# Handing the experts' rows over to the next mixer: weights requested early, row sums on DVE, the gate applied at the scatter, a fixed order, and the overflow block's second half under a branch

## The chip, the cores and the metric

The program runs on one core of a Trainium2 chip. The metric is device time in microseconds (us), from the start of the program to its end. The engines are TensorE (PE in the rows, PEld for its weight loads), VectorE (DVE), ScalarE (ACT), GpSimd (POOL) and SyncE (SP, which here only issues DMAs). Each works through its own list of instructions in order and waits for the others on semaphores.

## What is computed

Two stacked blocks of a transformer, all in float32. The first has two layers, each a mixer followed by a mixture of experts; then comes a norm, and then a second block of its own two mixers, each followed by a convolutional feed-forward net. The parts that matter here:

```python
def modulate(x, g, shift, scale):
    return rmsnorm(x, g) * (1 + scale) + shift
...
for l in range(DEPTH):                       # DEPTH = 2
    h_l = modulate(x_lat, norm_mix[l], sh1, sc1)     # and h_c for the context tokens
    o_c, o_l = mixer_ab(...) if l % 2 == 0 else mixer_na(...)
    x_lat = x_lat + g1 * o_l
    h_l = modulate(x_lat, norm_ffn[l], sh2, sc2)
    # layer 0: 256 context + 512 latent tokens; layer 1: the latent ones alone
    y = hier_moe(tokens, ...)                # 32 experts, 2 per token
    x_lat = x_lat + g2 * y[n_c:]             # context: x_ctx + g2c * y[:n_c]
return rmsnorm(x_lat, norm_final)            # then second_block, which begins with even_mixer
...
(jax.nn.silu(xb @ w_gate[e]) * (xb @ w_up[e])) @ w_down[e]      # one expert
```

## The kernel before

Tokens lie in tiles of 128 rows of 1024 in `xO`: tiles 0 and 1 are the context, 2 to 5 the latent tokens. `moe` runs a layer's experts. Each expert has up to 128 tokens gathered by an indirect DMA (`ex_load`), transposed (`ex_x`, L1227), multiplied by its up and gate weights (`ex_in`, L1218) in halves of 64 tokens, passed through silu and product (`ex_act`, L1240 on ACT, L1241 on DVE), transposed (L1251, copied by DVE, L1252), multiplied by the down weights, scaled by each token's weight `wl` (layer 0: ACT, L1259; layer 1: DVE, L1261, where the gate row `gain` is multiplied in too) and scattered to `Y` (L1262), which holds two rows for each token. `experts` runs the 32 in order; a branch (L1299) reads from `tix` whether an expert has over 64 tokens and takes the arm with both halves (`ex_rest`) or that with the first alone (`ex_out`). Weights come through a ring of slots (`wraw`, L110), twelve of 512 KB for an expert, requested by SyncE. Tokens beyond an expert's 128 rows go to overflow blocks, run by a hardware loop of `nov` passes (L1095), which always computes both halves; `nov` was 1 in layer 0 and 0 in layer 1 here. `gains`, at the end of `experts`, spreads rows over 128 partitions with matmuls (L403, copied at L404): the gate rows `G` in layer 0, the final norm's row in layer 1.

`finish` hands over to the next mixer: `tile(t)` loads a tile's pairs of rows (`yp`, L1114, by SyncE), adds the two rows of a token (L1116, GpSimd), multiplies by the gate in layer 0 (L1118, DVE) and adds to `xO` (L1119, DVE). In `mixer_na` `norm(t)` squares (L312, ACT), takes the root (L294, ACT, which needs a table of its own, hence a table load), the reciprocal (L295, DVE), scales (L315, DVE) to `h`, and turns `h` on TensorE (L1394 for the shift, L1395), split into a high half (L197, ACT) and a low half (L198, DVE); the values projection (L202 to L204) follows tile by tile, then the others. `final_norm` does the like for `even_mixer` (transposes at L1554). The mixers' weights pass through `wchunk`: L121 on ACT makes the high half, L122 on DVE the low one.

What sets the order: the program's order on each engine, except that a scheduler may move an instruction that isn't kept in place by `keep_in_program_order`. `warm` (L194) issues matmuls whose result nobody reads. The loop's branch and its end stand on every engine's list.

## Time and profile before

| | before |
|---|---|
| median of 3 runs | 3548.57 us (3546.37 to 3550.68) |
| the profiled execution | 3547.91 us |
| its span | 3546.1 us |
| TensorE busy | 3280.6 us (93%) |
| DVE, ACT, GpSimd busy | 1464.9, 1052.8, 499.1 us |
| experts of layer 0 | about 622 to 1196 us |
| experts of layer 1 | about 1655 to 2181 us |

The profile is of one execution. Busy time is a mean over stages with different limits: in most of the experts the weights' DMAs set the pace, in the mixers TensorE does. What a change at one place is worth is read there, from which wait ends last.

### The profile page before, as it was taken

Reading aid. Unit: us, or ns where it says so; the run is one execution under the profiler, and the core shown is the slowest. Engines: PE = TensorE matmul, PEld = TensorE weight load, DVE = VectorE, ACT = ScalarE, POOL = GpSimd, SP = SyncE. Lnnn points to the kernel's source line nnn. Section 1 sums busy time; section 2 is a strip of 40 time slices with the busy share of each in tenths; the row PEclk is TensorE's granted clock in tenths of the full one; section 3 lists DMA queues with packets and bytes.
Section 4 is the critical chain, followed back from the end, with each engine's and each line's share of the span. In section 5 each row is a group of like instructions: output and inputs, shape, how many; then the busy total and the mean of one; then the engine's idle time right before and its main releaser. Section 6 shows DMA issues by size and latency. Waiting matters only on the chain. (4 is left out here: it accounts for less than half of the span.)

```text
span 3546.1 us, 44389 instructions
## 1 busy us (share of the span) xinstructions
PE 3280.6 (93%) x16488; PEld 2125.4 (60%) x16488; DVE 1464.9 (41%) x2831; ACT 1052.8 (30%) x1948; POOL 499.1 (14%) x581
## 2 busy tenths in 40 slices
PE   7999988999988799998988886999999999999998
PEld 5954556333322487765332222876888888788887
DVE  4476565211111455565211113427443456355344
ACT  3465541111111244451000001326332334333232
POOL 1044421111110223321111112103000000000000
PEclk9999999999999799999999998999999999999999
DMA  5134465998999422236999996323333344233331
GB/s 201 54 123 133 159 214 200 351 408 315 378 398 388 172 72 77 66 131 237 406 401 395 395 391 224 119 89 91 89 97 99 84 62 95 72 101 103 95 98 45
DMA packets 351078, 676.27 MB, mean 191 GB/s; under 512 B 43029, under 2 KB 194773, under 8 KB 349409
## 3 DMA queue, kind: packets, MB, share of 16 engines
q1 hardware_dynamic: 313816, 626.50, 50.3%
q0 software_dynamic: 17584, 25.94, 2.1%
q10 hardware_dynamic: 19416, 20.34, 1.9%
q8 instruction: 165, 2.70, 0.3%
q14 instruction: 97, 0.79, 0.1%
HBM read 676.74 MB, written 29.45 MB: 199 GB/s over the span
## 5 line engine op out<-in xcount | busy, mean ns | idle before, releaser
L1218 PE MATMUL ea<-wr,xT 128*64 128x512 f32 x2368 | 622.1, 603 | 47.8 <-DMA wr<-in_moe_w_up_dram 26.5
L122 DVE TENSOR_TENSOR wh<-wr,wh 128x1024 fp32r<-128x1024 f32 (+2 forms) x276 | 339.1, 1235 | 314.1 <-ACT wh L121 313.4
L202 PE MATMUL aw<-hh,wh 128*128 128x512 f32 (+1 forms) x1216 | 441.9, 364 | 3.7 <-ACT wh L121 2.6
L203 PE MATMUL aw<-hl,wh 128*128 128x512 f32 (+1 forms) x1216 | 442.5, 364 | 1.8 <-DVE hl L198 1.8
L204 PE MATMUL aw<-hh,wh 128*128 128x512 f32 (+1 forms) x1216 | 441.3, 364 | 0.0
L1218 PEld LDWEIGHTS ea<-wr,xT 128*64 128x64 f32 x2368 | 183.6, 137 | 427.7 <-issue 311.2
L121 ACT CAST wh<-wr 128x1024 fp32r<-128x1024 f32 (+2 forms) x276 | 281.3, 1027 | 433.5 <-PE acc L204 288.1
L1218 PE MATMUL ea<-wr,aT 128*64 128x512 f32 x1184 | 282.4, 619 | 44.2 <-DVE aT L1252 39.0
L203 PEld LDWEIGHTS aw<-hl,wh 128*128 128x128 f32 x1216 | 231.2, 190 | 40.0 <-issue 3.5
L202 PEld LDWEIGHTS aw<-hh,wh 128*128 128x128 f32 x1216 | 230.7, 190 | 40.9 <-ACT wh L121 3.5
L204 PEld LDWEIGHTS aw<-hh,wh 128*128 128x128 f32 x1216 | 231.0, 190 | 38.0 <-issue 3.5
L472 POOL TENSOR_TENSOR pp<-pp,rc 128x768 f32<-128x768 f32 (+3 forms) x192 | 211.7, 1110 | 259.1 <-DVE rc L471 244.9
L1218 PEld LDWEIGHTS ea<-wr,aT 128*64 128x64 f32 x1184 | 83.4, 141 | 188.0 <-issue 130.3
L1262 POOL DMA_INDIRECT Y<-ey,idx x74 | 74.7, 1010 | 859.9 <-ACT ey L1259 434.0
L470 ACT ACTIVATE pp<-s,nm 128x768 f32<-128x768 f32 (+3 forms) x192 | 137.1, 716 | 156.5 <-DVE nm L1486 79.5
L202 PE MATMUL acc<-wh,hh 128*128 128x512 f32 (+2 forms) x480 | 177.2, 369 | 0.0
L203 PE MATMUL acc<-wh,hh 128*128 128x512 f32 (+2 forms) x480 | 175.8, 366 | 0.0
L204 PE MATMUL acc<-wh,hl 128*128 128x512 f32 (+2 forms) x480 | 175.5, 366 | 0.0
L1252 DVE COPY aT<-pt 128x256 f32<-128x256 f32 x74 | 31.4, 424 | 329.1 <-PE pt L1251 329.1
L1228 ACT COPY xT<-pt 128x512 f32<-128x512 f32 x65 | 37.9, 583 | 388.4 <-PE pt L1227 376.1
L1228 DVE COPY xT<-pt 128x512 f32<-128x512 f32 x65 | 44.9, 691 | 248.8 <-PE pt L1227 248.8
L1240 ACT ACTIVATE sg<-ea 64x256 f32<-64x256 f32 x148 | 55.7, 376 | 300.7 <-PE ea L1218 248.8
(480 smaller groups left out, 5251.6 us busy)
## 6 DMA issues: line engine op xcount, KB each, us to landing
wr<-in_moe_w_gate_dram SPq DMA_DIRECT2D x260, 512.0 KB
wr<-in_moe_w_up_dram SPq DMA_DIRECT2D x260, 512.0 KB
wr<-in_moe_w_down_dram SPq DMA_DIRECT2D x260, 512.0 KB
wr<-in_w_ada_dram SPq DMA_DIRECT2D x96, 512.0 KB
wr<-in_ffn_w_up_dram SPq DMA_DIRECT2D x88, 512.0 KB
wr<-in_ffn_w_down_dram SPq DMA_DIRECT2D x44, 512.0 KB
wr<-in_odd_w_in_dram SPq DMA_DIRECT2D x32, 512.0 KB
wr<-in_na_w_in_dram SPq DMA_DIRECT2D x30, 512.0 KB
```

The source lines that it names most:

```text
L121: keep(self.nc.scalar.copy(hi, raw))
L122: keep((self.lo_eng or self.nc.vector).tensor_sub(lo, raw, f(hi)))
L202: mm(ps, ah, bh, start=first, stop=False)
L203: mm(ps, ah, bl, start=False, stop=False)
L204: mm(ps, al, bh, start=False, stop=last)
L470: nc.scalar.activation(p[:, :n], s[:, b:b + n], AF.Exp, bias=nm, scale=sign, accum_out=rc)
L472: nc.gpsimd.tensor_mul(p[:, :n], p[:, :n], rc.broadcast_to([P, n]))
L1218: self.tc.keep_in_program_order(self.nc.tensor.matmul(*a, **k))
L1228: (self.nc.vector.tensor_copy if g else self.nc.scalar.copy)(x[:, g * 4:g * 4 + 4, :], pt.rearrange("p (k t) -> p k t", t=P))
L1240: self.nc.scalar.activation(sg[64:, c], a[:64, c], AF.Silu)
L1252: nc.vector.tensor_copy(at, pt[:, :256].rearrange("p (k t) -> p k t", k=4))
L1262: nc.gpsimd.indirect_dma_start(Y.rearrange("t (h d) -> (t h) d", h=2), bass.IndirectOffsetOnAxis(ap=idx[:, h], axis=0), y, None, bounds_ch ...
```

## The change

- `overflow()` is called inside `experts` at the last one: it reads `nov`, requests the overflow block's weights under a branch, and then requests the first weight chunks of the next mixer (three for `mixer_na`, four for `even_mixer`), so that they stand ahead of the last branches on SyncE's list.
- The overflow block stands under `If(nov > 0)` and has the two arms of an expert; further blocks are a loop under `If(nov > 1)`.
- In layer 0 the gate is applied before the scatter: `ctx` says for each row whether its token is of the context, `dgain` is the difference of the two gate rows, and DVE does two products in place of ACT's one. `gains` spreads the next norm's rows there in place of the gate rows, and the spread after the loop is gone. `shift_scale` is done at the fourth expert.
- The two rows of a token are added by DVE; four `yp` loads are issued at once. `table` loads the root's table ahead.
- The norms of `mixer_na` and `even_mixer` are taken apart (`square`, `scale`, `turn`) and their instructions on DVE, ACT, TensorE and SyncE are kept in program order (they all show as line L52). Six `warm` matmuls stand ahead of the first turn: in `mixer_na` behind the first `add` (they read its result), in `even_mixer` ahead of all adds.

```diff
+class Pinned:
+    def __init__(self, tc, eng):
+        self.tc, self.eng = tc, eng
+    def __getattr__(self, name):
+        fn = getattr(self.eng, name)
+        def call(*a, **k):
+            return self.tc.keep_in_program_order(fn(*a, **k))
+        return call
...
+    def table(self, fn):
+        t = self.sm.tile([P, 1], F32, name="tab")
+        self.nc.scalar.activation(t, self.eps[EPS], fn)
...
-        if self.gain is None:
-            nc.scalar.mul(y, acc, wl[:, h])
-        else:
-            nc.vector.scalar_tensor_tensor(y, acc, wl[:, h], self.gain, ALU.mult, ALU.mult)
+        wl, ctx = wl
+        gain = self.gain
+        if ctx is not None:
+            gain = y
+            nc.vector.scalar_tensor_tensor(y, self.dgain, ctx[:, h], self.gain, ALU.mult, ALU.add)
+        nc.vector.scalar_tensor_tensor(y, acc, wl[:, h], gain, ALU.mult, ALU.mult)
...
             def gains():
                 if l:
                     self.gfin = self.spread(pg, src, 8, ps, "xg1")
-                    return
-                for i, w in enumerate(ws):
-                    G[w] = self.spread(pg, src, 8 * i, ps, f"xg{i}")
-            past = self.past(nt, sc["K"], idx, tix, wl, eid, px, ps, off)
+                else:
+                    self.nA = {w: self.spread(pg, self.nmod[0], 16 * w + 8, ps, f"xg{i}") for i, w in enumerate(ws)}
+            past = self.past(nt, sc["K"], idx, tix, wl, eid, px, ps, off, ctx)
             def first():
-                self.both(idx[:, :, :NE], slf, ps, off)
+                self.both(idx[:, :, :NE], slf, ps, off, None if l else ctx[:, :, :NE])
...
+            def overflow():
+                nov = nc.values_load(eid[0:1, NOB:NOB + 1], min_val=0, max_val=NOB)
+                ev = nc.sync.value_load(eid[0:1, 0:1], min_val=0, max_val=NE - 1)
+                self.n = RING - 1
+                with tc.If(nov > 0):
+                    w = self.ex_load_w(l, ev)
                 self.n = -1
-                self.shift_scale()
-            with tc.For_i(0, nov, 1):
-                ev = nc.sync.value_load(eid[0:1, 0:1], min_val=0, max_val=NE - 1)
-                self.expert(l, ev, idx[:, :, NE:NE + 1], wl[:, :, NE:NE + 1], xo, Y, T, px, ps)
-                for a, w0 in ((tix, NE), (idx[:, 0], NE), (idx[:, 1], NE), (eid, 0), (wl[:, 0], NE), (wl[:, 1], NE)):
-                    sh = px.tile([P, NOB - 1], a.dtype, name="sh", tag="sh")
-                    nc.vector.tensor_copy(sh, a[:, w0 + 1:w0 + NOB])
-                    nc.vector.tensor_copy(a[:, w0:w0 + NOB - 1], sh)
-                self.ex_load(tix[:, NE:NE + 1], xo, hD, T)
+                self.raws = [self.wraw(s) for s in then]
+                return nov, w
+            nov, w = self.experts(l, tix, idx, wl, ctx, xg, hD, Y, T, px, ps,
+                                  [first] + past + ([] if l else [self.shift_scale]), gains, overflow)
+            with tc.If(nov > 0):
+                self.ex_block(w, xo, slots, px, ps, nc.values_load(tix[64:65, NE:NE + 1], min_val=0, max_val=int(BIG)))
+            self.n = RING + 11
+            with tc.If(nov > 1):
+                with tc.For_i(1, nov, 1):
+                    for a, w0 in ((tix, NE), (idx[:, 0], NE), (idx[:, 1], NE), (eid, 0), (wl[:, 0], NE), (wl[:, 1], NE),
+                                  *([] if l else [(ctx[:, 0], NE), (ctx[:, 1], NE)])):
+                        sh = px.tile([P, NOB - 1], a.dtype, name="sh", tag="sh")
+                        nc.vector.tensor_copy(sh, a[:, w0 + 1:w0 + NOB])
+                        nc.vector.tensor_copy(a[:, w0:w0 + NOB - 1], sh)
+                    self.ex_load(tix[:, NE:NE + 1], xo, hD, T)
+                    ev = nc.sync.value_load(eid[0:1, 0:1], min_val=0, max_val=NE - 1)
+                    self.ex_block(self.ex_load_w(l, ev), xo, slots, px, ps)
...
-            def tile(t):
-                y = py.tile([P, 2, D], F32, name="yp", tag="yp")
-                nc.sync.dma_start(y, Y[2 * t * P:2 * (t + 1) * P, :].rearrange("(p k) d -> p k d", k=2))
-                a = y[:, 0, :]
-                nc.gpsimd.tensor_add(a, a, y[:, 1, :])
-                if G:
-                    nc.vector.tensor_mul(a, a, G[who_of(t)])
-                nc.vector.tensor_add(xO[:, t0 + t, :], xO[:, t0 + t, :], a)
-                return y[:, 1, :]
-            return tile
+            def load(t):
+                y[t] = py.tile([P, 2, D], F32, name="yp", tag="yp")
+                self.nc.sync.dma_start(y[t], Y[2 * t * P:2 * (t + 1) * P, :].rearrange("(p k) d -> p k d", k=2))
+            def add(t):
+                a, x = y[t][:, 0, :], xO[:, t0 + t, :]
+                self.nc.vector.tensor_add(a, a, y[t][:, 1, :])
+                self.nc.vector.tensor_add(x, x, a)
+                return y[t][:, 1, :]
+            return load, add
...
+        gains()
+        return over
+    def ex_block(self, w, xg, out, px, ps, more=None):
         x = self.ex_x(xg, px, ps)
         a = ps.tile([P, 512], F32, name="ea", tag="b")
         self.ex_in(a, w, x, 0, range(8))
-        self.ex_rest(w, x, self.ex_act(a, px), (idx, wl, Y, T, px, ps), px, ps)
+        self.ex_arms(more, w, x, self.ex_act(a, px), out, px, ps)
...
+    def ex_arms(self, more, w, x, sg, out, px, ps):
+        if more is None:
+            return self.ex_rest(w, x, sg, out, px, ps)
+        with self.tc.If(more < out[3]) as many:
+            self.ex_rest(w, x, sg, out, px, ps)
+        with many.Else():
+            self.ex_out(w, sg, 0, *out)
...
+                    nA, parts, sel = self.nmod
+                    load, add = finish(e3, ps) if finish else (None, None)
                     pn = e3.enter_context(self.pool(name="nan", bufs=1, side="right"))
+                    with self.pinned():
+                        self.table(AF.Sqrt)
+                        for t in range(4 if add else 0):
+                            load(t)
+                        self.prefetch(self.na_first())
+                        A = self.nA or {w: self.spread(pn, nA, 16 * w + 8, ps, f"A{w}") for w in (1, 0)}
+                        bank[0] = lambda: ps.tile([P, 512], F32, name="aw", tag="b")
+                        first = values(0, range(NT))
+                        hs, ss, junk = {}, {}, {}
+                        def square(t):
+                            hs[t] = pn.tile([P, D], F32, name="h", tag="h", bufs=2)
+                            ss[t] = self.sm.tile([P, 1], F32, name="ss")
+                            self.nc.scalar.activation(junk.get(t, hs[t]), xO[:, t, :], AF.Square, accum_out=ss[t])
+                            self.nc.scalar.activation(ss[t], ss[t], AF.Sqrt, bias=self.eps[EPS], scale=1.0 / D)
+                        def scale(t):
+                            self.nc.vector.reciprocal(ss[t], ss[t])
+                            self.nc.vector.scalar_tensor_tensor(hs[t], xO[:, t, :], ss[t], A[1 if t < 2 else 0], ALU.mult, ALU.mult)
+                        def turn(t, g):
+                            w = 1 if t < 2 else 0
+                            c = slice(t * P, (t + 1) * P)
                             pt = ps.tile([P, 512], F32, name="pt", tag="b")
 ...
+                            self.nc.scalar.copy(hh[:, g:g + 4, c], v)
+                            return lambda: self.nc.vector.tensor_sub(hl[:, g:g + 4, c], v, f(hh[:, g:g + 4, c]))
+                        for t in range(NT + 2):
+                            if add and t < NT:
+                                junk[t] = add(t)
+                                if 0 < t < 3:
+                                    load(t + 3)
+                            if add and t == 0:
+                                self.warm(ps, xO[:, 0, 0:512], 6)
+                            low = []
+                            if 0 < t <= NT:
+                                low.append(turn(t - 1, 0))
+                            if t < NT:
+                                square(t)
+                            if 0 < t <= NT:
+                                low.pop()()
+                                low.append(turn(t - 1, 4))
+                            if t < NT:
+                                scale(t)
+                            if low:
+                                low.pop()()
+                            if t > 1:
+                                first[t - 2]()
...
+                        load, square, scale, turn, back = self.final_norm(pe, xO, hh, hl, ps, finish)
+                        pe.enter_context(self.pinned())
+                        self.table(AF.Sqrt)
+                        for t in range(4):
+                            load(t)
+                        self.prefetch(self.even_first())
+                        self.warm(ps, xO[:, 2, 0:512], 6)
...
                         if (i, j) == (0, 0):
-                            tile(0)
-                            tile(1)
-                        elif (i, j) == (0, 2):
-                            tile(2)
+                            for t in (0, 1):
+                                square(t)
+                            for t in (0, 1):
+                                scale(t)
+                            for t in (0, 1):
+                                turn(t)
+                            for t in (2, 3):
+                                square(t)
+                            for t in (2, 3):
+                                scale(t)
+                        elif (i, j) == (0, 3):
+                            turn(2)
```

What the change moves, at three places. First DVE in an expert of layer 0, from the products of its first half on: `sg` is the product, `aT` the transposed copy, `ey` the scaled output, a branch chooses between both halves (the rows up to the next branch) and the first alone. Before:

```order
L1241 TENSOR_TENSOR sg<-sg,ea 64x256 x2
L1298 TENSOR_LOAD tix
L1299 COMPARE_AND_BRANCH
L1252 COPY aT<-pt 128x256
L1241 TENSOR_TENSOR sg<-sg,ea 64x256 x2
L1252 COPY aT<-pt 128x256
L1299 UNCONDITIONAL_BRANCH
L1252 COPY aT<-pt 128x256
L1299 UNCONDITIONAL_BRANCH
```

After:

```order
L1298 TENSOR_TENSOR sg<-sg,ea 64x256 x2
L1359 TENSOR_LOAD tix
L1376 COMPARE_AND_BRANCH
L1319 SCALAR_TENSOR_TENSOR ey<-dgain,ctx,gain 128x512 x2
L1309 COPY aT<-pt 128x256
L1298 TENSOR_TENSOR sg<-sg,ea 64x256 x2
L1320 SCALAR_TENSOR_TENSOR ey<-ea,wl,ey 128x512
L1309 COPY aT<-pt 128x256
L1320 SCALAR_TENSOR_TENSOR ey<-ea,wl,ey 128x512
L1376 UNCONDITIONAL_BRANCH
L1319 SCALAR_TENSOR_TENSOR ey<-dgain,ctx,gain 128x512
L1309 COPY aT<-pt 128x256
```

The gate rows (L1319) now stand ahead of the first `aT`, and the first half's scaling (L1320) between the two halves' `aT`.

Second, SyncE at the end of layer 0's overflow: `yp` the pairs of rows, `wr` raw weights. Before, from the loop's end on:

```order
L1095 REGISTER_ALU
L1095 COMPARE_AND_BRANCH
L1095 UNCONDITIONAL_BRANCH
L1114 DMA yp<-Y_5611 128x2048
L110 DMA wr<-in_na_w_in_dram 128x4x256 x2
L110 DMA wr<-in_na_w_in_dram 128x8x128
L1114 DMA yp<-Y_5611 128x2048 x5
```

After, first at the last expert, where the overflow's requests end, then from the loop's end on:

```order
L1139 UNCONDITIONAL_BRANCH x2
L1137 ISA x2
L144 DMA wr<-in_na_w_in_dram 128x4x256 x2
L144 DMA wr<-in_na_w_in_dram 128x8x128
L1359 TENSOR_LOAD tix
L1359 ISA x2
```

```order
L1150 COMPARE_AND_BRANCH
L1150 UNCONDITIONAL_BRANCH
L1149 UNCONDITIONAL_BRANCH
L52 DMA yp<-Y_5611 128x2048 x5
L144 DMA wr<-in_na_w_in_dram 128x8x128 x2
```

The next mixer's first weights have moved ahead of the experts' last branch (L1376), and the `yp` loads stand in a row.

Third, DVE from there on: `h` the normed tile, `A` and `xg` the spread norm rows, `hl` the low half of a turned tile. Before:

```order
L404 COPY A_11448<-mrow 128x512
L404 COPY A_11461<-mrow 128x512
L1118 TENSOR_TENSOR yp<-yp,xg_11157 128x1024
L1119 TENSOR_TENSOR xO<-xO,yp 128x1024
L122 TENSOR_TENSOR wh<-wr,wh 128x1024 x3
L295 RECIPROCAL ss<-ss 128x1
L315 SCALAR_TENSOR_TENSOR h<-xO,ss,A_11448 128x1024
L1118 TENSOR_TENSOR yp<-yp,xg_11157 128x1024
L1119 TENSOR_TENSOR xO<-xO,yp 128x1024
```

After:

```order
L52 TENSOR_TENSOR wh<-wr,wh 128x1024 x3
L52 TENSOR_TENSOR yp<-yp 128x1024
L52 TENSOR_TENSOR xO<-xO,yp 128x1024
L52 RECIPROCAL ss<-ss 128x1
L52 SCALAR_TENSOR_TENSOR h<-xO,ss,xg_11350 128x1024
L52 TENSOR_TENSOR yp<-yp 128x1024
L52 TENSOR_TENSOR xO<-xO,yp 128x1024
L52 TENSOR_TENSOR hl<-pt,hh 128x4x128
L52 RECIPROCAL ss<-ss 128x1
```

The weights' subtractions come ahead of the first sum, each tile has two sums and no gate product, and tile 1's sums stand behind tile 0's scaling.

## Rows read from the trace of the kernel before

**Rows 1.** Windows: stretch, length, busy us of PE, PEld, DVE, ACT, POOL, PEclk, DMA share, GB/s.

```profile
800.00:920.00 120.00, 115.29 (x567) 40.98 (x564) 16.47 (x35) 17.25 (x36) 16.73 (x17) 1.00 0.85 316
920.00:1150.00 230.00, 203.91 (x856) 68.20 (x855) 27.93 (x57) 26.83 (x56) 26.45 (x26) 1.00 1.02 397
...
1262.00:1300.00 38.00, 37.96 (x230) 33.02 (x229) 22.28 (x46) 16.81 (x30) 13.22 (x17) 1.00 0.32 96
```

**Rows 2.** Timeline of layer 0's overflow block: start, us, engine, line, operation, [idle <-releaser].

```profile
1167.65 8.60 PE L1218 MATMUL ea<-wr,xT 128*64 128x512 f32 x32 [0.24 <-ACT xT L1228]
...
1177.57 0.42 DVE L1241 TENSOR_TENSOR sg<-sg,ea 64x256 f32<-64x256 f32 x1 [0.44 <-ACT sg L1240]
...
1183.05 0.46 PE L1251 MATMUL pt<-c_ident,sg 64*128 64x64 f32 x4
...
1184.02 3.65 PE L1218 MATMUL ea<-wr,aT 128*64 128x512 f32 x16 [0.52 <-DVE aT L1252]
...
1193.25 0.97 POOL L1262 DMA_INDIRECT Y<-ey,idx  x1 [3.51 <-ACT ey L1259]
...
1196.24 0.34 SPq L1114 DMA_DIRECT2D yp<-Y  x1
```

**Rows 3.** DMA of the stretch 1193 to 1196.2 us, the second half's scatter.

```profile
DMA packets 80, 0.00 MB, mean 0 GB/s; under 512 B 80, under 2 KB 80, under 8 KB 80
```

**Rows 4.** Timeline, layer 0's first rows and the first norm.

```profile
1202.08 2.34 POOL L1116 TENSOR_TENSOR yp<-yp 128x1024 f32<-128x1024 f32 x1 [7.86 <-DMA yp<-Y]
...
1206.07 1.23 DVE L1119 TENSOR_TENSOR xO<-xO,yp 128x1024 f32<-128x1024 f32 x1
...
1207.38 1.06 ACT L312 ACTIVATE yp<-xO 128x1024 f32<-128x1024 f32 x1 [1.29 <-DVE xO L1119]
...
1209.49 1.28 ACT L294 ACT_TABLE_LOAD   x1
1210.78 0.29 ACT L294 ACTIVATE ss<-ss,eps 128x1 f32<-128x1 f32 x1
...
1216.18 0.80 PE L1395 MATMUL pt<-c_ident,h 128*128 128x128 f32 x2 [11.46 <-DVE h L315]
```

**Rows 5.** Lines of the stretch 1216 to 1262 us: DVE's low-half subtraction, busy, mean ns.

```profile
L198 DVE TENSOR_TENSOR hl<-pt,hh 128x512 fp32r<-128x512 f32 x12 | 8.3, 688 | 7.5 <-ACT hh L197 7.5
```

**Rows 6.** Timeline of TensorE: one tile's turn and values, and the first projection.

```profile
1246.52 0.23 PE L1394 MATMUL pt<-nsel,nparts 96*128 96x128 bf16 x1
...
1252.08 0.23 PE L1394 MATMUL pt<-nsel,nparts 96*128 96x128 bf16 x1
...
1260.51 0.40 PE L202 MATMUL aw<-hh,wh 128*128 128x512 f32 x1
```

**Rows 7.** Timeline of layer 1's handover.

```profile
2174.57 3.65 PE L1218 MATMUL ea<-wr,aT 128*64 128x512 f32 x16 [0.79 <-DVE aT L1252]
...
2179.30 0.98 POOL L1262 DMA_INDIRECT Y<-ey,idx  x1 [3.86 <-DVE ey L1261]
...
2182.97 0.33 SPq L1114 DMA_DIRECT2D yp<-Y  x1
...
2188.10 2.33 POOL L1116 TENSOR_TENSOR yp<-yp 128x1024 f32<-128x1024 f32 x1 [7.82 <-DMA yp<-Y]
...
2195.65 1.28 DVE L315 SCALAR_TENSOR_TENSOR fh<-xO,ss,xg 128x1024 f32<-128x1024 f32 x1
...
2196.99 1.97 PE L1554 MATMUL pt<-c_ident,fh 128*128 128x128 f32 x8 [16.79 <-DVE fh L315]
...
2213.08 0.58 PE L203 MATMUL aw<-hl,wh 128*128 128x256 f32 x1 [1.62 <-DVE hl L198]
```

**Rows 8.** The scatter's line in layer 0; DVE's scaling line, min/median/max ns.

```profile
600.00:1164.00 564.00, 37.37 (x38) 0.99 0.95 369
...
L1261 DVE SCALAR_TENSOR_TENSOR ey<-ea,wl,gain x34: 749/751/753, 1670.3 to 2178.3; 128x512 f32<-128x512 f32 x34
```

**Rows 9.** The experts' branch on GpSimd's queue, min/median/max ns.

```profile
L1299 POOLq INC_SWDGE_SEM  x56: 390/1508/2680, 630.6 to 2162.8; - x56
```

More of the change, by code (lines that the diff above doesn't have):

```diff
@@ L1 @@
 import math
-from contextlib import ExitStack
+from contextlib import ExitStack, contextmanager
 import numpy as np
@@ L1198, in fill @@
                 v.tensor_copy(t, acc)
-                self.both(dst[:, :, NE:], t, ps, o)
+                self.both(dst[:, :, NE:], t, ps, o, ctx[:, :, NE:] if ctx is not None and o is not None else None)
         return [count, blocks, fill]
@@ L1271, in ex_rest, with experts @@
         self.ex_out(w, sg2, 1, *out)
-    def experts(self, l, tix, idx, wl, xg, hD, Y, T, px, ps, past, gains):
+    def experts(self, l, tix, idx, wl, ctx, xg, hD, Y, T, px, ps, past, gains, overflow):
         nc = self.nc
@@ L1286, in experts @@
                 w1 = self.ex_load_w(l, e + 1)
+            else:
+                over = overflow()
             self.ex_in(a, w, x, 0, range(2, 5))
@@ L1562, in back @@
                 nc.gpsimd.dma_start(xO[:, t, :], xD[t * P:(t + 1) * P, :])
-        return tile, back
+        return load, square, scale, turn, back
     def ln_rows(self, pool, l, j):
@@ L1683, in even_mixer @@
                             self.to_feat(xO[:, t, :], hh, hl, t, ps)
[L1684 removed]
+                        load = square = scale = turn = back = lambda *t: None
                     else:
[L1686 to L1687 removed]
+                        load, square, scale, turn, back = self.final_norm(pe, xO, hh, hl, ps, finish)
[5 more added lines that the diff above has]
+                        self.warm(ps, xO[:, 2, 0:512], 6)
                     out = []
@@ L2068, in program @@
                 with ExitStack() as pe:
-                    tile, back = self.final_norm(pe, xO, hh, hl, ps, finish)
+                    load, square, scale, turn, back = self.final_norm(pe, xO, hh, hl, ps, finish)
                     for t in range(4):
-                        tile(t)
+                        load(t)
+                        square(t)
+                        scale(t)
+                        turn(t)
                     back()
```

129 lines of the change are left out of this document (67 added, 62 removed).

## Prediction, made before the changed kernel ran

> **What bounds the kernel now.** I read the windows first, then the timelines of the two places where the experts hand over to the next mixer, then the lines that price the new instructions. The windows show that most of the program is closed to this change: in 800 to 920 us of layer 0 TensorE is busy 115.29 of 120 us, in 920 to 1150 the DMA engines are full (share 1.02), and once the next mixer is under way TensorE is busy 37.96 of 38 us [rows 1]. What is open lies between these stretches. In layer 0 the overflow block's last scatter starts at 1193.25 and SyncE asks for the first pair of expert rows (yp) at 1196.24 [rows 2]; the rows land when GpSimd's add starts at 1202.08, and TensorE does next to nothing until its first turn of a normed tile at 1216.18, after 11.46 us of idleness put down to DVE's h [rows 4]. The first projection proper starts at 1260.51 [rows 6]. In layer 1 the last scatter is at 2179.30, yp is asked for at 2182.97 and landed at 2188.10, TensorE sits 16.79 us until 2196.99, and its dense work starts at 2213.08 [rows 7]. From there on everything hangs on TensorE, so what a handover gains moves the end.
>
> **The change part by part.**
>
> *Layer 0, overflow block (term A).* The block computes both halves although the second holds nothing: its scatter at 1193.25 moved 0.00 MB in 80 packets, all under 512 B [rows 3]. Under the new branch the second half goes. By the rows: its up and gate matmuls for one half are the first 32, 1167.65 + 8.60 = 1176.25; ACT and DVE follow and end with the product at 1177.57 + 0.42 = 1177.99, today hidden behind the second half's matmuls, then on the path; from the transposes to the output matmuls 1184.02 - 1183.05 = 0.97, and 3.65 for these [rows 2]: 1182.6. The scaling moves from ACT to DVE at 0.75 [rows 8], and a scatter follows it by 0.3: 1183.8. Request after scatter took 1196.24 - 1193.25 = 2.99 [rows 2], so 1186.8. One more level of branches stands on the way, with an added semaphore instruction on GpSimd's queue ahead of SyncE's first yp request; the like takes 0.39 to 2.68 us, median 1.51 [rows 9]. Part of that lies beside the scatter's landing; I take 0.8, bounds 0 and 3.0 (two of them in a row). The request is then at 1187.6, and A = 1196.24 - 1187.6 = **8.6** (6.4 to 9.4). The early weights go over queues that are idle then and cost nothing; if their slots were late, SyncE would hold the overflow weights and A would shrink.
>
> *Layer 0, norm stage (term C).* From landing to projection today: 1260.51 - 1202.08 = 58.4 [rows 4, 6]. Landing stays 1202.08 - 1196.24 = 5.8 behind the request, so the new landing T is at 1193.4. Removed are the 32 spreads after the landing's request, GpSimd's add (2.34), the gate product, and the table load ahead of the first square root (1.28) [rows 4]; DVE gets one add instead. The weight subtractions that stood between the first add and the reciprocal are done before T. The new order, in time from T: two adds of 1.23, 2.5; square on ACT 1.06, the read of its sum and the root 0.29 [rows 4], to 4.2; the small reciprocal and the scaling of 1.28 [rows 7], to 5.8. But six warm-up matmuls, 24 instructions, stand on TensorE behind the first add and ahead of the first turn: 24 x 3.65/16 = 5.5 at full clock [rows 2], twice that at half. TensorE comes from some 13 us of idleness, so I take 7.3, between the two, to T + 9.8. ACT's copy of the turned tile stands ahead of the second tile's square, so tile 1 is scaled only at T + 15.2. After that DVE and ACT take turns: 2.5 for the adds, 1.6 for square and root, 1.5 for reciprocal and scaling, 0.7 for a low-half subtraction [rows 5] and some 0.3 of hand-offs, 6.6 a tile, longer than TensorE's 1252.08 - 1246.52 = 5.56 [rows 6]. Tile 5 is scaled at 15.2 + 4 x 6.6 = 41.6, and with its turn and values (5.56), the copies between them and tile 4's values the stage ends at T + 50. C = 58.4 - 50 = **8.4**; if the chain kept up with TensorE, 13; if the fixed order saved nothing, 0.
>
> *The table switch.* The load took 1.28 and the root started at 1210.78, the moment it ended [rows 4]; C and D go by that. The Trainium skill (ScalarE: Activation LUTs, section What ACT_TABLE_LOAD costs) gives about 1.28 us for the load and another 1.38 of drain, 2.66 for each switch; by that the sum would be up to 2.8 us better over both layers, but the rows show no such drain here.
>
> *Layer 1 (term D).* No overflow block ran. The request gets the same extra branches: I take 0.5 (bounds 0 and 3.0) on 2182.97, landing 5.13 later as now [rows 7]: T = 2188.6. Both first adds run before any scaling: 4.9; ACT's square and root of tile 0 lie beside the second add; scaling of tiles 0 and 1 ends at T + 6.5 and T + 8.0. Two turns of 1.97 [rows 7] reach T + 10.5, copies and subtractions of the last half T + 12.3 = 2200.9. Today dense work starts at 2213.08: 12.2 earlier. The warm-up runs here well before the rows land, so the clock may be low again; I take **11.5**, bounds 6 (second yp late) and 14.
>
> *Experts (term E).* In layer 0 each half gets two DVE instructions of 0.75 [rows 8] for one on ACT. The first depends on no matmul and runs beside them. The second stands ahead of the second half's transposed copy where an expert has two halves; where that is so today (layer 1) TensorE waits 0.79 instead of 0.52 [rows 2, 7], 0.27 more. Layer 0 scatters 38 halves for its 32 experts [rows 8], so six have two, most in 800 to 920, where TensorE is the bound: 1.6. In the other stretches weights bound and hide it. The new spreads at the first expert lie there too. I take **+1.5**, bounds 0 and 5.
>
> *Sum.* -8.6 - 8.4 - 11.5 + 1.5 = -27.0. The profiled execution took 3547.91, which is 0.66 under the median of 3548.57; on the median the forecast is 3521.6, **3521**. The good bounds together give -36, the bad ones about -10.
>
> **The rivals.**
>
> *The fixed order gives back what it saves (C = 0).* Warm-up and in-order ACT hold tile 1 so long that the norm stage stays at 58.4. For it: the first turn moves from T + 14 only to T + 10. Against: DVE's 3-us instructions beside GpSimd's adds go. C is 0 and D half: -8.6 - 6 + 1.5 = -13, 3535.
>
> *The branches cost more.* A skipped level makes the queues wait and count. At the longest 2.68 [rows 9] for two levels in both layers, 10.7 instead of the 1.3 taken: -17.6, 3531. The Trainium skill (Runtime: NRT & Kernel Launch, section Instruction fetch mechanics) says that a taken branch out of the fetched window stalls the engine for a fetch; it gives no price, and the rows hold none to be told from the semaphore's.
>
> *The second half is not skipped* (its flag would read as if it had tokens). Then A is near 0 or below: -18.4, 3530. The empty scatter speaks against it [rows 3].
>
> *Slower: the gate on DVE holds every output.* Place: layer 0's 38 halves [rows 8]. If DVE, in order, could not write the gate row because its buffer still feeds the last scatter, or did both products on the path, each half would cost TensorE 2 x 0.75 [rows 8]: 38 x 1.5 = 57 less the 28.5 gained: +28.5, 3577. It decides from 0.75 a half on, which is one of the products in full. Against: the buffers are two deep, so a half waits for the last scatter but one, and after 920 TensorE has slack (203.91 of 230) [rows 1].
>
> **How the numbers follow.** Forecast 0.62 (3512 to 3530); fixed order 0.16; branches 0.07; second half 0.04; DVE gate 0.08, of which 0.02 ends within the bound; other losses 0.03. The range for 8 in 10 reaches from the good bound to just past the first rival: 3512 to 3537. Measurements of this kernel tell some 0.2%, 7 us, from no change. Faster by more: 0.62 + 0.13 (fixed order, but for its worst) + 0.07 + 0.04 = 0.86; within: 0.03 + 0.02 + 0.01 = 0.06; slower: 0.06 + 0.02 = 0.08.
>
> **What would show it.** A: one scatter of the overflow block, near 1184, and yp asked for near 1187.6. C: no GpSimd add, DVE adds at 1.2 us, first projection 50 us behind the landing with 6.6 us between tiles, against 58 in the rival. D: dense matmuls near 2201 less the layer 0 gain. E: 800 to 920 longer by no more than 2 us. Branches: time from last scatter to yp request over 4 us. The prediction is wrong if the experts of layer 0 lengthen by more than 5 us, or if the stretch after the handover no longer keeps TensorE at full clock and busy.

## The result and the profile after

| | before | after |
|---|---|---|
| median | 3548.48 us (3546.37 to 3550.68) | 3519.43 us (3519.27 to 3527.55) |
| ratio | | 0.992 (95%: 0.9908 to 0.9932) |
| profiled execution, its span | 3547.91, 3546.1 us | 3519.27, 3517.5 us |
| TensorE, DVE, ACT, GpSimd busy | 3280.6, 1464.9, 1052.8, 499.1 us | 3270.0, 1515.1, 1027.7, 468.3 us |

The forecast was 3521, and 29 us were gained. But the sum came out for partly wrong reasons: two errors of about the same size cancel in it. The rows below are of the changed kernel. Timeline rows give start, us, engine, line, operation and in brackets the idle time before it with what ended it.

The timeline of layer 0's last expert and its overflow block, to answer to [rows 2] and [rows 4]:

```profile
1158.67 0.97 POOL L1321 DMA_INDIRECT Y<-ey,idx  x1 [18.07 <-DVE ey L1320]
1165.32 0.75 DVE L1319 SCALAR_TENSOR_TENSOR ey<-dgain,ctx,gain 128x512 f32<-128x512 f32 x1 [5.48 <-DMA Y<-ey,idx]
1166.11 0.42 DVE L1309 COPY aT<-pt 128x256 f32<-128x256 f32 x1
1166.63 5.00 PE L1275 MATMUL ea<-wr,aT 128*64 128x512 f32 x16 [6.40 <-issue]
...
1172.70 0.97 POOL L1321 DMA_INDIRECT Y<-ey,idx  x1 [13.06 <-DVE ey L1320]
...
1193.20 0.97 POOL L1321 DMA_INDIRECT Y<-ey,idx  x1 [19.52 <-DVEq L1149]
1198.01 8.97 SPq L52 DMA_DIRECT2D yp<-Y  x5
1202.91 1.23 DVE L52 TENSOR_TENSOR yp<-yp 128x1024 f32<-128x1024 f32 x1 [4.33 <-DMA yp<-Y]
...
1251.56 0.40 PE L240 MATMUL aw<-hh,wh 128*128 128x512 f32 x1
```

The overflow block scatters once, as forecast, but `yp` is asked for at 1198.01, not at 1187.6: later than before (1196.24). DVE's gate row (L1319) stood 5.48 us still until a scatter had landed, the copy `aT` (L1309) stood behind it, and TensorE behind that. By the view of line L1319 (what DVE waited for ahead of it: us, times) this was one of 21 such waits:

```profile
  DMA Y<-ey,idx: 41.2, 21
```

What stood between that scatter and the request, by the instructions of the branches on GpSimd's queue (count, min/median/max ns, first and last start):

```profile
L1376 POOLq INC_SWDGE_SEM  x1: 2080/2080/2080, 1193.0 to 1193.0; - x1
```
```profile
L1149 POOLq INC_SWDGE_SEM  x1: 2088/2088/2088, 1195.8 to 1195.8; - x1
```

These are two in a row of the kind of [rows 9], one for each level of branches. The first projection (the last row of the timeline) follows at 1251.56, before at 1260.51 [rows 6].

The timeline of the second handover, to answer to [rows 7]:

```profile
2169.02 2.16 SPq L52 DMA_DIRECT2D yp<-Y  x4
...
2171.28 7.81 PE L52 MATMUL warm<-xO,c_ident 128*128 128x512 f32 x12 [4.97 <-issue]
2184.28 1.94 PE L52 MATMUL pt<-c_ident,fh 128*128 128x128 f32 x8 [5.20 <-DVE fh L52]
2186.01 1.91 PE L52 MATMUL pt<-c_ident,xg 128*128 128x128 f32 x8
...
2188.47 0.58 PE L52 MATMUL aw<-hl,wh 128*128 128x256 f32 x1
```
```profile
2176.04 1.22 DVE L52 TENSOR_TENSOR yp<-yp 128x1024 f32<-128x1024 f32 x1
2179.12 1.23 DVE L52 TENSOR_TENSOR xO<-xO,yp 128x1024 f32<-128x1024 f32 x1 [1.86 <-PE warm L52]
```

`yp` is asked for at 2169.02 and dense work starts at 2188.47: 19.45 us, before 30.11. DVE's second instruction waits 1.86 us for the warm-up matmuls, which read the tile that it writes.

One gain stands where no instruction that the forecast spoke of had changed. Windows of layer 1's experts, before and after (length; busy PE, PEld, DVE, ACT, POOL; granted clock, which is the share of full speed that TensorE was given; DMA share; GB/s):

```profile
1700.00:1800.00 100.00, 90.96 (x456) 33.76 (x456) 20.04 (x46) 9.38 (x21) 15.15 (x16) 0.98 1.03 406
```
```profile
1700.00:1800.00 100.00, 92.00 (x420) 33.30 (x421) 18.36 (x34) 8.62 (x19) 13.72 (x14) 0.98 1.03 415
```

The DMA engines are full in both (1.03), yet move 415 GB/s in place of 406. Layer 1's experts, from first scatter to last, took 501.2 us in place of 507.9; a second trace of each kernel shows 502.5 and 508.4.

### The profile page after: what moved, and what is told of

Same layout as the page of the kernel before. It is cut to its first block, busy times and chain, and to the rows that moved or that the text cites. A ratio compares the mean times of both kernels' runs of the same rounds, so it can differ in the third digit from the quotient of the medians.

```text
span 3517.5 us, 44393 instructions
## 1 busy us (share of the span) xinstructions
PE 3270.0 (93%) x16460; PEld 2118.1 (60%) x16460; DVE 1515.1 (43%) x2899; ACT 1027.7 (29%) x1908; POOL 468.3 (13%) x569
## 5 line engine op out<-in xcount | busy, mean ns | idle before, releaser
L1275 PE MATMUL ea<-wr,xT 128*64 128x512 f32 x2336 | 607.5, 601 | 38.5 <-DMA wr<-in_moe_w_up_dram 21.8
L157 DVE TENSOR_TENSOR wh<-wr,wh 128x1024 fp32r<-128x1024 f32 (+2 forms) x269 | 328.8, 1228 | 308.9 <-ACT wh L156 308.2
L240 PE MATMUL aw<-hh,wh 128*128 128x512 f32 (+1 forms) x1184 | 432.1, 366 | 2.9 <-ACT wh L156 2.6
L241 PE MATMUL aw<-hl,wh 128*128 128x512 f32 (+1 forms) x1184 | 432.7, 366 | 0.0
L242 PE MATMUL aw<-hh,wh 128*128 128x512 f32 (+1 forms) x1184 | 431.4, 365 | 0.0
L156 ACT CAST wh<-wr 128x1024 fp32r<-128x1024 f32 (+2 forms) x269 | 274.2, 1027 | 417.6 <-PE acc L242 287.4
L240 PEld LDWEIGHTS aw<-hh,wh 128*128 128x128 f32 x1184 | 223.9, 189 | 39.7 <-ACT wh L156 3.5
L242 PEld LDWEIGHTS aw<-hh,wh 128*128 128x128 f32 x1184 | 224.1, 189 | 37.6 <-issue 3.5
L242 PE MATMUL acc<-wh,hl 128*128 128x512 f32 (+2 forms) x480 | 176.1, 367 | 0.0
L241 PE MATMUL acc<-wh,ah 128*128 128x512 f32 x352 | 137.8, 392 | 0.0
L1298 DVE TENSOR_TENSOR sg<-sg,ea 64x256 f32<-64x256 f32 x146 | 62.0, 425 | 175.7 <-ACT sg L1297 173.0
```

Of the source, the lines that this page charges most:

```text
L156: keep(self.nc.scalar.copy(hi, raw))
L157: keep((self.lo_eng or self.nc.vector).tensor_sub(lo, raw, f(hi)))
L240: mm(ps, ah, bh, start=first, stop=False)
L241: mm(ps, ah, bl, start=False, stop=False)
L242: mm(ps, al, bh, start=False, stop=last)
L1275: self.tc.keep_in_program_order(self.nc.tensor.matmul(*a, **k))
```

## The experiments

Medians with their spread, ratios to the kernel before on the same chip (its medians 3547.4 to 3549.0). Executions of one kernel on one chip lie up to 10 us apart, so where little is at stake the trace decides; each trace is of one execution. The kernels before and after were run again beside the others: 3550.06 (one run) and 3518.96 (3512.73 to 3522.30), ratio 0.9911 (0.9894 to 0.9928).

**What held the overflow block: the buffer or the branch.** The gate row goes to a buffer of its own.

```diff
-            gain = y
-            nc.vector.scalar_tensor_tensor(y, self.dgain, ...)
+            gain = px.tile([P, 512], F32, name="eg", tag="eg", bufs=1)
+            nc.vector.scalar_tensor_tensor(gain, self.dgain, ...)
```

> The gate row gets a tile of its own (eg) in place of being written into the scatter's buffer ey; nothing else changes against the changed kernel (3519.4 us). Theory A (buffer): the last expert's output matmuls start late (1166.6 us in the changed kernel, 1157.4 before) because DVE, in order, stands at the gate row until the scatter of expert 30 has landed, 6.6 us after its start at 1158.7, and the transposed copy stands behind it. Then the output matmuls start near 1161.2, the yp rows are asked for some 5 us earlier (near 1192.6) and the time is 3513 to 3515. Rival B (branches): TensorE's wait there is the added branches and register loads themselves; then no change, 3518 to 3520.

3514.05 (3511.65 to 3515.99), ratio 0.9904 (0.9887 to 0.9920). Its timeline at the same place:

```profile
1157.22 0.97 POOL L1321 DMA_INDIRECT Y<-ey,idx  x1 [17.96 <-DVE ey L1320]
1158.86 0.75 DVE L1319 SCALAR_TENSOR_TENSOR eg<-dgain,ctx,gain 128x512 f32<-128x512 f32 x1 [0.47 <-DVE sg L1298]
1159.64 0.42 DVE L1309 COPY aT<-pt 128x256 f32<-128x256 f32 x1
...
1166.58 0.97 POOL L1321 DMA_INDIRECT Y<-ey,idx  x1 [8.38 <-DVE ey L1320]
```

From scatter to scatter 9.36 us in place of 14.03 (before 8.96). `yp` is asked for at 1192.19, 5.8 us sooner. It was the buffer: the gate row is written into a tile that scatters read, and so DVE waited for a scatter ahead of it. The branches alone don't hold `aT`.

**The gate back behind the sum,** as in the kernel before, all else as changed.

```diff
-        nc.vector.scalar_tensor_tensor(y, acc, wl[:, h], gain, ALU.mult, ALU.mult)
+        if gain is None:
+            nc.scalar.mul(y, acc, wl[:, h])
...
+                    self.nc.vector.tensor_mul(a, a, G[who_of(t)])
```

> Undoes the gate at the scatter in layer 0 alone: ACT scales by the token's weight, DVE multiplies by the gate after the sum of the two rows, the gate rows are spread at the end of the experts and the norm rows after the overflow block. Theory A: the last expert's wait (5.4) and the experts' lengthening (2.8 us between first and 31st scatter) go, but each tile's chain gets 1.2 us, six times, and the norm rows' spread of 7.2 us lies beside the landing: 3517 to 3521. Rival B (the wait was the branches): the experts change by 1.6 at most and the norm stage loses 6: 3523 to 3526.

3514.99 (3511.10 to 3516.01), ratio 0.9908 (0.9891 to 0.9924), a little better than either theory. The experts are 8.2 us earlier by the last but one (1150.48 against 1158.67) and the request 13.0 (1184.99), but from the request to the first projection it takes 59.7 us in place of 53.6: the product stands in each tile's chain again. (The norm's rows are spread there too, but are there at 1187.7, ahead of the landing at 1189.78.) The projection starts at 1244.69: 6.9 us sooner than in the changed kernel, and 1.4 sooner than with a buffer for the gate row (1246.04). So moving the gate gained nothing: with the shared buffer it cost 6.9 us, with its own it comes out about even.

**The warm-ups.** None in the first norm stage; those of the second read a tile that no sum writes at that time.

```diff
-                            if add and t == 0:
-                                self.warm(ps, xO[:, 0, 0:512], 6)
```
```diff
-                        self.warm(ps, xO[:, 2, 0:512], 6)
+                        self.warm(ps, xO[:, 5, 0:512], 6)
```

> Leaves out the six warm-up matmuls ahead of mixer_na's first turn. Theory A: they hold the chain of tiles, since ACT's copy of the turned tile 0 stands ahead of tile 1's square; without them the first turn starts 6 us behind the first sum's start instead of 10, tile 1 is scaled 3 to 4 us earlier, and the low clock of the first turns costs part of it back: 3516 to 3519. Rival B: the clock they raise is worth more than the wait, the first two tiles and the first values run at half clock: 3521 to 3526.

> even_mixer's warm-up matmuls read tile 5 of xO in place of tile 2, whose sum is the first to be written. Theory A: DVE's first sum into xO waited 1.86 us for these matmuls (start 2179.1, its input ready at 2177.3), and everything up to the dense matmuls hangs on it: 1.8 us less, 3517.6. Rival B: the wait is covered by the second tile's chain: no change, 3519.4.

Without the first: 3513.03 (3512.80 to 3514.41), ratio 0.9902 (0.9886 to 0.9919); request to projection 52.38 us in place of 53.55. The first two turns run at a granted clock of 0.50, the lower of its two levels, and still nothing is lost. The stage shows 1.2 us of the 6 by which this median is lower; where the others come from is not shown. With the second reading elsewhere: 3517.58 (3516.28 to 3524.63), ratio 0.9921 (0.9904 to 0.9937); request to dense work 17.61 us in place of 19.45, that is the 1.86 us wait and no more, too little for the medians to show. The wait doesn't arise in every execution: in the traces without the first warm-ups and of the next experiment the second warm-ups start ahead of the request, DVE's sum finds them done, and the stretch takes 18.15 and 17.72 us with the tile unchanged. TensorE stood 2.2 and 1.8 us ahead of them there and 4.97 in the changed kernel; the reason is not shown.

**The second half of the overflow block, computed again.**

```diff
-  self.ex_block(w, xo, slots, px, ps, nc.values_load(tix[64:65, NE:NE + 1], ...))
+  self.ex_block(w, xo, slots, px, ps)
```

> The overflow block computes both halves again, without a branch; all else as in the changed kernel. Theory A (the half is worth what the rows say): 7.1 us of up and gate matmuls and 4.5 between the scatters come back, 1.7 of the first half's product are hidden again, and one level of branches with its 2.05 us on GpSimd's queue goes: the yp rows are asked for 6 to 9 us later, 3526 to 3528. Rival B (the skipped half's wait, its branch and its semaphore instruction ate the gain): 3518 to 3521.

3523.76 (3520.50 to 3528.12), ratio 0.9934 (0.9918 to 0.9951), between the two forecasts. The half is skipped by the change, and was worth some 5 us. Computed again, it scatters a second time, 8.3 us after the change's only scatter, and `yp` is asked for at 1204.25, 6.2 later:

```profile
1196.68 0.97 POOL L1321 DMA_INDIRECT Y<-ey,idx  x1 [22.63 <-DVE ey L1320]
1201.52 0.97 POOL L1321 DMA_INDIRECT Y<-ey,idx  x1 [3.87 <-DVEq L1149]
```

Without the block's two arms one level of branches and one semaphore instruction are left, and the request comes 2.73 us after the scatter, not 4.81: that level costs 2.08 us.

**The row sums back on GpSimd.**

```diff
-                self.nc.vector.tensor_add(a, a, y[t][:, 1, :])
+                self.nc.gpsimd.tensor_add(a, a, y[t][:, 1, :])
```

> GpSimd adds the two rows of a token again, in both layers; all else as in the changed kernel. Theory A: its 2.3 to 3.3 us a tile stand ahead of the first tile, and DVE's adds and scalings beside it take up to 3.2 us instead of 1.2: the stretch from yp's request to the first projection grows from 53.6 to 58 or more in layer 0, and layer 1's to the dense matmuls by 2 to 3: 3525 to 3530. Rival B: GpSimd runs ahead of a chain that the fixed order paces, and takes 1.2 us a tile off DVE: 3515 to 3519.

3521.85 (3519.16 to 3524.53), ratio 0.9922 (0.9906 to 0.9939). The time lies between the two forecasts. Request to projection in layer 0: 53.3 us, as on DVE. In layer 1 request to dense work takes 21.7 in place of 19.45. The engine of the sums is worth some 2 us, in layer 1 alone.

**The fixed order undone:** the scheduler may move the norm stages' instructions.

```diff
-        self.nc = InOrder(self.tc, nc)
```

> The changed kernel without the fixed order: the instructions of the two norm stages stand as in the changed program, but the scheduler may move them as before. Theory (the fixed order is what keeps the chain of a tile at 6 us): from the request for yp to the first projection in layer 0 53.6 us rises to 58 to 60, in layer 1 from 19.5 us to dense work to 22 to 27; time 3519 rises to about 3530. Rival (what was taken out gives the gain, the order itself nothing): 53.6 and 19.5 within 1 us, 3519 within 3.

3517.18 (3512.30 to 3519.08), ratio 0.9914 (0.9901 to 0.9928). From request to projection it took 48.8 us, not 58 to 60: 4.7 less than in the fixed order. In layer 1 22.4, 2.9 more. So the theory fell: the fixed order as such gives nothing over both stages together. Where it loses is seen on ACT, first with the fixed order, then without:

```profile
1205.48 1.06 ACT L52 ACTIVATE yp<-xO 128x1024 f32<-128x1024 f32 x1 [8.53 <-DVE xO L52]
...
1214.69 0.59 ACT L52 CAST hh<-pt 128x512 fp32r<-128x512 f32 x1 [7.73 <-PE pt L52]
1215.18 1.06 ACT L52 ACTIVATE yp<-xO 128x1024 f32<-128x1024 f32 x1
```
```profile
1204.86 1.06 ACT L1470 ACTIVATE yp<-xO 128x1024 f32<-128x1024 f32 x1 [10.87 <-DVE xO L1175]
...
1207.52 1.04 ACT L1470 ACTIVATE yp<-xO 128x1024 f32<-128x1024 f32 x1
```

The scheduler squares tile 1 right behind tile 0; in the fixed order the square stands behind the copy of tile 0's turn, 7.73 us of waiting.

**Where the weights lie.** After the change the slots of the weight ring begin at byte 22784 of each partition, before at 22592: `table` takes a small buffer (`tab`, six copies) from a pool that lies ahead of the ring. All other variants above share the new place. Two kernels shift the ring alone: the kernel before by 192 bytes (to 22784), the changed one by 64 (to 22848).

```diff
+        self.cp.tile([P, 48], F32, name="shift")
```
```diff
+        self.cp.tile([P, 16], F32, name="shift")
```

> The kernel before, with nothing added but an unused buffer of 192 bytes per partition ahead of the weight ring. It moves every slot of the ring from byte 22592 on to byte 22784 on, where the changed kernel has it (there a small buffer that the change adds shifts it). Theory (the gain in the weight-bound stretches, 508 us to 501 from layer 1's first scatter to its last, comes from where the slots lie): layer 1's stretch falls to 501 us, DMA in 1700 to 1800 us rises from 406 to about 415 GB/s, layer 0 gains about 3 us, and the time falls from 3549 to about 3539. Rival (that gain comes from the changed instructions): 508 us, 406 GB/s, 3549 within noise.

> The changed kernel, with nothing added but an unused buffer of 64 bytes per partition ahead of the weight ring, which moves its slots from byte 22784 (a multiple of 256) to 22848 (64 past a multiple of 128, as the slots of the kernel before are). Theory (the place of the slots sets the rate): layer 1's stretch from first to last scatter rises from 501 to 508 us, the rate falls to about 407 GB/s, the time rises from 3519 to about 3529. Rival (the changed instructions set it): 501 us, 415 GB/s, 3519. If the rate follows where the slots lie, but by another rule than the multiple of 128, the first of these two runs gains and this one doesn't lose.

Before, shifted: 3535.95 (3530.82 to 3540.66), ratio 0.9965 (0.9952 to 0.9977). Changed, shifted: 3537.10 (3531.87 to 3539.32), ratio 0.9970 (0.9958 to 0.9982). The same windows, in that order:

```profile
1700.00:1800.00 100.00, 90.94 (x456) 33.49 (x454) 19.25 (x40) 8.79 (x20) 14.21 (x14) 0.98 1.03 416
```
```profile
1700.00:1800.00 100.00, 91.28 (x452) 33.29 (x448) 19.71 (x43) 8.77 (x20) 13.95 (x15) 0.97 1.03 406
```

Layer 1's experts take 502.6 and 507.5 us. The place sets the rate, whatever the instructions are: 415 GB/s with slots at a multiple of 256 bytes, 406 with slots 64 past one. No other place was run, so whether it takes a multiple of 256 or a smaller one would do is not shown. An unused buffer makes the kernel before 11.5 us faster; with its slots as badly placed as before, the change is worth 3547.41 - 3537.10 = 10.3 us, and with both well placed 3535.95 - 3518.96 = 17.0 (two chips). The times went beyond the forecasts, by 3 and 8 us; the second is taken up under what stays open. The Trainium skill (DMA: Bandwidth & Descriptors, section How a descriptor splits into AXI transactions) says that a descriptor is cut into transactions of 256 bytes that must start at multiples of 256, and that one which starts elsewhere pays for bytes that it doesn't use. For 4 KB and a start 64 bytes past, an estimate by that page is 130 beats in place of 128, 1.6%; the runs show 2.2%, on the writing side, of which the page gives no example.

**Everything that was found, together:** the gate row's own buffer, no first warm-up, the second on another tile, and layer 1's constant `aid` kept where the program loads it. The scheduler had put that load into layer 0's fourth expert, where SyncE's weight requests waited for it:

```profile
SPq L144 <- DMA c_aid<-const_aid_dram: 16.2, 1, 16.2
```

That is the view of the waits of the changed kernel; before, the wait was 11.0 us.

```diff
-            K["aid"] = self.const(f"aid{nt}", [P, 2, nt, 2], pk)
+            K["aid"] = pk.tile([P, 2, nt, 2], F32, ...)
+            tc.keep_in_program_order(nc.scalar.dma_start(K["aid"], self.C[f"aid{nt}"]))
```

> The changed kernel with four edits: the gate row in a buffer of its own; no warm-up matmuls in the first norm stage; those of the second read a tile that no add writes; and the constant aid of layer 1 is loaded where the program has it, and not at layer 0's fourth expert, where its completion held SyncE's weight requests for 16.2 us (11.0 in the kernel before). Theory (that hold is why layer 0's experts are 5 us late at the tenth): no such hold, tenth expert's scatter at about 807 to 808, later ones 5 us earlier, time 3503 to 3508. Rival (TensorE bounds these experts, and the weights catch up anyway): tenth expert at 812, time 3511 to 3513.

3506.30 (3503.91 to 3510.68), ratio 0.9881 (0.9866 to 0.9896): faster than both kernels, and in the range of the theory. But the theory on `aid` fell. The wait is gone and DMA moves 416 GB/s in 660 to 670 us in place of 69, yet from the first scatter to the thirteenth it takes 178.6 us, exactly as with the gate row's buffer alone (178.6). TensorE had weights enough. The gain over the first experiment is that of the warm-ups (request to projection 50.2 us, to dense work 17.7) and what runs differ by. In this trace layer 0's first scatter comes at 638.44, against 633.78 in the first experiment; whether the moved load has a part in that was not tried.

## What the gate costs the early experts

If not the weights, what? From the first scatter to the thirteenth it takes 175.2 us in the kernel before at the ring's new place, and 179.4 after. With the gate back behind the sum it is 176.1, with the gate row in its own buffer 178.6: so it is the gate's instructions in the experts, and hardly the buffer. TensorE's lines of that stretch (count | busy us, mean ns | idle before, by releaser), before:

```profile
L1219 PE MATMUL ea<-wr,xT 128*64 128x512 f32 x398 | 102.9, 604 | 3.4 <-DMA wr<-in_moe_w_up_dram 2.0 <-DMA wr<-in_moe_w_gate_dram 1.4
L1219 PE MATMUL ea<-wr,aT 128*64 128x512 f32 x192 | 43.8, 598 | 6.9 <-DVE aT L1253 5.6 <-issue 1.2
...
L1252 PE MATMUL pt<-c_ident,sg 64*128 64x64 f32 x48 | 5.9, 236 | 1.3 <-DVE sg L1242 1.3
```

And after:

```profile
L1275 PE MATMUL ea<-wr,xT 128*64 128x512 f32 x404 | 97.8, 596 | 0.0
L1275 PE MATMUL ea<-wr,aT 128*64 128x512 f32 x192 | 51.4, 684 | 10.1 <-DVE aT L1309 9.2 <-issue 0.9
...
L1308 PE MATMUL pt<-c_ident,sg 64*128 64x64 f32 x48 | 6.5, 244 | 2.6 <-DVE sg L1298 2.6
```

Waits for the copy `aT` are 3.6 us longer, waits for the product `sg` 1.3, the two groups of matmuls together 2.5 (146.7 to 149.2), and 3.4 of waiting for weights are gone: 4.0 of the 4.2. One expert with a single half shows the waits, in the kernel before as it was and after:

```profile
683.42 0.42 DVE L1252 COPY aT<-pt 128x256 f32<-128x256 f32 x1 [0.48 <-PE pt L1251]
683.95 3.65 PE L1218 MATMUL ea<-wr,aT 128*64 128x512 f32 x16 [0.62 <-issue]
```
```profile
689.04 0.75 DVE L1319 SCALAR_TENSOR_TENSOR ey<-dgain,ctx,gain 128x512 f32<-128x512 f32 x1 [0.28 <-DVE sg L1298]
689.82 0.42 DVE L1309 COPY aT<-pt 128x256 f32<-128x256 f32 x1
690.30 5.35 PE L1275 MATMUL ea<-wr,aT 128*64 128x512 f32 x16 [1.15 <-DVE aT L1309]
```

The gate row stands between the product and the copy. TensorE waits 1.15 us in place of 0.62, and the 16 matmuls behind the longer wait take 5.35 us in place of 3.65; the granted clock of 690 to 700 us is 0.83. Of four groups behind such waits (1.14 to 1.52 us) three took 5.29 to 5.35; with the gate back behind the sum all twelve groups of the stretch take 3.65. That the longer wait lowers the clock is argued from this pairing; no run changed the wait alone, and the wait right ahead doesn't decide it. A fifth group of the changed kernel is slow behind a short wait (granted clock of 670 to 680 us: 0.66), and so is the last expert's second group in the kernel before (1155 to 1165 us: 0.83):

```profile
672.84 6.14 PE L1275 MATMUL ea<-wr,aT 128*64 128x512 f32 x16 [0.52 <-DVE aT L1309]
```
```profile
1157.36 5.26 PE L1218 MATMUL ea<-wr,aT 128*64 128x512 f32 x16 [0.72 <-issue]
```

## Why the prediction was right, and where it was not

With the kernel before taken at the ring's new place (span 3534.6), the stages can be set side by side without the rate:

| stage | before, shifted | after | difference | forecast |
|---|---|---|---|---|
| start to the last but one expert's scatter | 1151.95 | 1158.67 | +6.7 | E: +1.5 |
| from there to the `yp` request | 39.87 | 39.34 | -0.5 | A: -8.6 |
| request to first projection | 64.46 | 53.55 | -10.9 | C: -8.4 |
| mixer, layer 1's experts, next request | 917.64 | 917.46 | -0.2 | 0 |
| request to dense work | 30.04 | 19.45 | -10.6 | D: -11.5 |
| the rest | 1330.64 | 1329.03 | -1.6 | 0 |
| span | 3534.6 | 3517.5 | -17.1 | -27.0 |

The rows for A and E together missed by 13 us, and the place of the ring, of which the forecast knew nothing, gave 11.5 by the spans. So the number 3521 was luck: two things that nobody forecast cancel. C and D, 20 of the 27 us, came as worked out; A and E did not.

- *A, the overflow block.* The half is skipped: computed again, its scatter comes 8.3 us later than the change's only one, where the rows gave some 9. Two steps failed. The sum began at the old start of the block, 1167.65, as if what precedes it were unchanged: but at the last expert the gate row's buffer put a scatter's landing in TensorE's way (the first experiment gives 4.4 us back at the request). And the branches put two instructions of 2.08 us ahead of the request, 4.81 us from scatter to request in place of 2.99; 0.8 was taken, the bound of 3.0 held.
- *C, the norm stage.* Right. From landing to projection it took 48.65 us, forecast 50, before 58.4; DVE's sums took 1.23 each, the tiles some 6.2 us in place of 6.6. The landing came another 0.9 us sooner. Of the 10.9 us the gate product is some 6 (they came back with it); which of the other removals gives the rest was not tried. The rival that the fixed order gives back what it saves is refuted as it was put, since C is not 0; but the order saves nothing either, it costs 4.7 us here.
- *The table switch.* The prediction counted the load's 1.28 us and no drain, and the traces agree. In the changed kernel the root follows the read of the square's sum at once (1206.44 + 0.19 to 1206.66). In the scheduler's order, where the load stands between them, the read ends at 1206.01 and the root starts at 1207.32.
- *D, layer 1.* Right: 10.6 of 11.5, and without the warm-up's hold it would have been more. The extra branches cost nothing here, where 0.5 was taken: scatter to request 3.62 us, before 3.67. One semaphore instruction of a skipped level stands there before (1.12 us) and after (1.09), since the block and its arms are skipped together. The stall of a taken branch that the Trainium skill speaks of (Runtime: NRT & Kernel Launch, Instruction fetch mechanics) isn't seen in that time.
- *E.* The mechanism that was costed is there: at the second half TensorE waits 0.79 in place of 0.52. What was missed stands in the order ahead of the prediction: in the arm with one half, too, the gate row stands before the copy. "The first depends on no matmul and runs beside them" is true of its inputs and not of its place on DVE's list. With the longer waits and the slower matmuls E is 4.8 at the thirteenth scatter and 6.7 at the last but one, over the bound of 5. From the first scatter to the last but one it is 6.1 (519.2 to 525.3), and more than 5 there was one of the two signs by which the prediction called itself wrong; the first two traces, with the ring at different places, hide it (524.0 to 525.3).
- *The rivals.* The one that ends slower named the right mechanism, the gate row waiting for its buffer. It did at 21 of 39 halves, 41.2 us of DVE's time; but nearly all of that lies where weights set the pace, and by the first experiment little more than the last, 5.5 us, is seen in the end. What spoke against it, "a half waits for the last scatter but one", isn't so: from 928 us to the last expert the row starts, sixteen times, 5.7 to 7.4 us after the scatter just before it. The buffers are two deep, but the program as built gives the first half of every expert the same one. That the second half isn't skipped is refuted by the rows above. That branches cost more is refuted for layer 1; in layer 0 the time from scatter to request is over 4 us, the prediction's sign for it.
- *The rest of the program.* The forecast gave 0 to the weight-bound stretches. The place of the ring alone, by the shifted kernel before, gave 5.3 us in layer 1's experts and 4.8 in layer 0's.

What stays open: the shift of the changed kernel cost 18 us by the medians, of which the two layers' experts show some 9; the dense part behind was 6.3 us longer in that profile (1335.3 against 1329.0) at a granted clock of 0.97 in place of 0.99 (2300 to 2600 us), and whether the place has a part in that was not tried. Nor was it tried what the early weight requests alone are worth.

## What to carry to other kernels

Before crediting an edit, see what else it moved: a small buffer (here 192 bytes with its copies) can shift every buffer behind it, and a kernel whose DMA engines are full should try its weight slots at multiples of 256 bytes. An instruction with free inputs still costs where it stands on an in-order list, so put filler behind, not ahead of, the copy that TensorE waits for, and never into the source of a scatter in flight. Before keeping a warm-up or a fixed order, run the kernel without it. And when a forecast comes out, compare it stage by stage: errors can cancel.

## What the runs showed of the hardware

- DMA into SBUF at full load: 415 to 416 GB/s with slots at a multiple of 256 bytes, 406 to 407 with slots 64 bytes past one, in both kernels (1700 to 1800 us).
- A scatter issued under full weight traffic (413 GB/s in 1158 to 1166 us) held its source for 6.6 us (1158.67 to 1165.32), from the start of its issue to the row that overwrites the source; over sixteen such experts 5.7 to 7.4.
- The semaphore instruction that a skipped level of branches leaves on GpSimd's queue took 2.08 and 2.09 us at layer 0's handover, one for each level in series, and 1.09 at layer 1's; one level less brought the request 2.08 us nearer to the scatter.
- TensorE's 16 output matmuls took 3.65 us in all of the kernel before's groups of the early experts (waits of 0.5 to 0.7 us), and 5.3 in three of four cases behind waits of 1.1 to 1.5 us after; but also 5.26 behind 0.72 us at the last expert before and 6.14 behind 0.52 after, so the wait right ahead does not settle it.
